# A hybrid decoder layer on one core: input loaded in four column pieces, unread products in the idle front, one Strassen block of the first FFN made plain

## The chip, the core and the metric

The kernel runs on one core of a Trainium2 chip. A core has a matrix engine (PE in the profile; its weight loads are PEld), a vector engine (DVE), a scalar engine (ACT), a general engine (POOL) and queues that start DMA transfers (SP's, and ACT's own). Each engine works through its own list of instructions in order and waits on semaphores. The metric is the device time of one execution in microseconds (us); lower is better.

## The reference, cut to what matters

One layer step for a prompt group (512 tokens) and a sample group (8 sequences of 4 tokens), 544 rows of width 1024 in all, in float32:

```python
def _layer(x, pos, p, attn_cache, ml_state):
    x = x + 0.5 * _swiglu(_rmsnorm(x, p['ffn1_norm']), p['ffn1_w_gate'], p['ffn1_w_up'], p['ffn1_w_down'])
    h = _rmsnorm(x, p['mix_norm'])
    # one projection, dilated attention (8 heads), mLSTM (4 heads), output projection
    ...
    x = x + mix @ p['w_out']
    x = x + 0.5 * _swiglu(_rmsnorm(x, p['ffn2_norm']), p['ffn2_w_gate'], p['ffn2_w_up'], p['ffn2_w_down'])
    return x, att_state, (C, n, m)
```

The hidden width of both FFNs is 2816, which is 22 column tiles of 128.

## The kernel before

The activations lie transposed: eight tiles `x` (128 of the 1024 columns by 544 rows). A float32 product is made of three products of rounded halves: the weight tile is split into `whi` (a cast on ACT) and `wlo` (a subtraction on DVE), the activation into `xh` and `xl`, and PE computes `xh*whi`, `xl*whi` and `xh*wlo`, each in two halves of 272 columns. One tile of 128 inputs (a `k`) of one column tile is therefore a group of six PE products, and a plain column tile (a `Job`) has eight groups, 48 products. Gate and up of one column tile are two jobs.

Two neighbouring column tiles can instead be one `Fast` job: gate and up of both by a Strassen scheme of seven products of 2x2 blocks, 7 x 24 = 168 PE products where four plain jobs take 192. It needs operands of its own (`oh`, `ol`, made from sums `xn`, `xd` on DVE and ACT) and sums of weights (`ws` on DVE). `PLAIN = 4` is the number of column tiles at the start of an FFN that are plain.

The FFN goes in parts of 8, 8 and 6 column tiles. The first part of FFN 1 is therefore 8 plain jobs, 2 `Fast` jobs and 8 down jobs.

The order of instructions on every engine is written by a planner when the program is built: class `Order` keeps a planned time `t` and clocks of the engines, pieces of work are generators that yield the time from which they may go on, and `Engine.cost` gives the planned cost of an instruction. These planned times fix only the order; on the chip, semaphores decide when an instruction starts.

The front works like this. SP's queue loads `ident`, the norm gain, the input as `xt` (per half of the 1024 columns four row blocks of 128x512, and `xst` for the samples), and between the halves the first two gate columns (`wraw`, 512 KB each). PE turns the input into `x` tiles by products with `ident` (four of `xt` and one of `xst` per tile). `FastNorm.from_rows` computes sums of squares from the rows (`sj`), `scales` makes the row scales and spreads them with a product of `dg` by `onesd` into `rb`; the gate's and up's results are multiplied by `rb` when they leave PSUM. PSUM has two accumulators for jobs (`mm`) and four small ones (`aux`). The first two jobs run interleaved:

```python
first = [(j, slot()) for j in jobs[:2]]
for ks in (range(0, 4), range(4, 8)):
    for i, (j, ps) in enumerate(first):
```

Of the kernel before, what the change touches and what calls it, by code (L numbers as in the profile page):

```python
# [51 lines left out]
class Order:  # L52
# [132 lines left out]
class Engine:  # L185
# [5 lines left out]
    def cost(self, op, out, ins, kw):  # L191
        n = max([size(out)] + [size(a) for a in ins])
        sbuf = all(a.space == bass.MemoryType.SB for a in [out] + ins)
        if self.name == "dma":
            b = 4 * size(out) * out.shape[0]
            return max(0.1, b / (3.6e5 if self.order.t > 15.0 else 2.7e5))
# [48 lines left out]
def hybrid_layer_kernel(ctx: ExitStack, tc: tile.TileContext, I: dict, C: dict, O: list):  # L245
# [49 lines left out]

    ident = small("ident", (P, P))
    dma.dma_start(ident, C["ident"])
    nc.scalar.preload_act_table_set("natural_log_exp_and_others")
    od.table = 1
    gcol = small("gcol", (P, 32))  # L300
    grow1 = small("grow1", (KD, P))
    dma.dma_start(grow1, I["ffn1_norm"].rearrange("(m p) -> m p", p=P))
# [63 lines left out]
    class FastNorm(Norm):  # L366
# [6 lines left out]
        def from_rows(self, blocks):  # L373
            self.rows = True
            ssa, ssd = small("ssa", (P, 2, 2)), small("ssd", (P, 3, 2))
            v, y, t = (small(n, (P, CH + 1)) for n in ("rsv", "rsy", "rst"))
            pool.memset(ssd, 1.0)
            for c in range(2):
                xb, xs_ = blocks[c]
                for b, x in enumerate(xb + [xs_]):  # L380
                    yield R(x) - 0.2
                    n = NS if b == CH else P
                    j = t2("sj", (P, 512))
                    if b < 2:
                        act.activation(j[0:n], x, AF.Square, accum_out=ssa[:, b, c:c + 1])
                    else:
                        dve.tensor_tensor_reduce(out=j[0:n], in0=x, in1=x, scale=1.0, scalar=0.0, op0=OP.mult,
                                                 op1=OP.add, accum_out=ssd[0:n, b - 2, c:c + 1])
            od.spawn(self.scales(ssa, ssd, v, y, t), 0, R(ssa, ssd) - 0.2)

        def scales(self, ssa, ssd, v, y, t):
            dve.tensor_tensor(v[:, 0:2], ssa[:, :, 0], ssa[:, :, 1], op=OP.add)
            dve.tensor_tensor(v[:, 2:5], ssd[:, :, 0], ssd[:, :, 1], op=OP.add)
# [99 lines left out]
    class Raw:  # L493


        def __init__(self, w, r0, nk, cols, *more):
            self.w, self.cols = w, cols
            self.parts = [(r0, nk)] + list(more)
            self.nk = sum(n for _, n in self.parts)
            self.left = len(cols)  # L500
            self.t = None

# [4 lines left out]
        def load_cols(self):  # L507
            c0, n = self.cols[0], len(self.cols)
            together = all(c == c0 + i * P for i, c in enumerate(self.cols))
            k0 = 0  # L510
            for r0, nk in self.parts:
                rows = self.w[r0:r0 + nk * P]
                if together:
                    dma.dma_start(self.t[:, k0:k0 + nk, :n * P], rows[:, c0:c0 + n * P].rearrange("(k p) c -> p k c", p=P))
                else:
                    for i, c in enumerate(self.cols):
                        dma.dma_start(self.t[:, k0:k0 + nk, i * P:(i + 1) * P],
                                      rows[:, c:c + P].rearrange("(k p) c -> p k c", p=P))
                k0 += nk

    class Job:
        def __init__(self, raw, c, xs, after, start=True, stop=True, split=None):
# [3 lines left out]
            self.w = None  # L526

        def split(self):
            hi = wp.tile([P, 8, P], F32R, name="whi", tag="wsp", bufs=8)
            lo = wp.tile([P, 8, P], F32R, name="wlo", tag="wsp", bufs=8)  # L530
            nk = self.nk
            if self.custom:
                self.custom(hi, lo)
            else:
                src = self.raw.t[:, :nk, self.c * P:(self.c + 1) * P]
                act.copy(hi[:, :nk], src)
                yield R(hi) - 0.3
                dve.tensor_tensor(lo[:, :nk], src, hi[:, :nk].bitcast(F32), op=OP.subtract)
                self.raw.left -= 1
            self.w = (hi, lo)  # L540
# [61 lines left out]
    def run(jobs):  # L602
# [19 lines left out]
        def splitter():  # L622
            for n, j in enumerate(jobs):
# [23 lines left out]
        def products(j, ps, ks, hs=(0, 1)):  # L647
            od.need(lambda: j.w is not None)
            hi, lo = j.w
            for k in ks:  # L650
                od.need(lambda: j.xs(k) is not None)
# [40 lines left out]
        for ks in (range(0, 4), range(4, 8)):  # L692
            for i, (j, ps) in enumerate(first):
                for k in ks:
                    products(j, ps, (k,))
                    used[0] = max(used[0], k + 1)
                    od.poll()
                if 7 in ks:
                    finish(j, ps)
                    at[0], unit[0] = i + 1, pos[i + 1]  # L700
# [16 lines left out]
    def ffn_jobs(pre, get_norm, after):  # L717
        wg, wu, wd = I[pre + "_w_gate"], I[pre + "_w_up"], I[pre + "_w_down"]
        jobs = []
        for f0, f1 in zip(PARTS, PARTS[1:]):  # L720
# [4 lines left out]
            def gate(f, zg=zg):  # L725
                def post(ps, full):
                    z = t2("zg")
                    yield 0, 0, lambda: get_norm().rb is not None
                    dve.tensor_tensor(halves(z), ps, halves(get_norm().rb), op=OP.mult)
                    done(full, kind="mm")  # L730
# [13 lines left out]
            def up(f, zg=zg, hidden=hidden):  # L744
                def post(ps, full):
# [5 lines left out]
                    dve.tensor_tensor(z, zg[f], z, op=OP.mult)  # L751
                    yield from hidden(f, z)
# [65 lines left out]
            for f in range(0, nf, 2):  # L818
                c0 = (f0 + f) * P
                if f0 + f >= PLAIN:  # L820
# [7 lines left out]
                else:  # L828
                    jobs += [Job(Raw(wg, 0, 8, [cols[i]]), 0, xs, gate(f + i)) for i in range(2)]
# [22 lines left out]

    xp4 = I["x_prompt"].rearrange("(b p) d -> p b d", p=P)
    xsm = I["x_sample"].flatten_outer_dims()
    xin = []
    for c in range(2):
        xs_ = t2("xst", (NS, 512))
        blocks = []
        for b in range(CH):
            xb = t2("xt", (P, 512))  # L860
            dma.dma_start(xb, xp4[:, b, c * 512:(c + 1) * 512])
            blocks.append(xb)
        dma.dma_start(xs_, xsm[:, c * 512:(c + 1) * 512])
        xin.append((blocks, xs_))
        if c == 0:
            jobs[0].raw.load()
            jobs[1].raw.load()
    jobs[2].raw.load()

    def start():  # L870
# [5 lines left out]
        for c in range(2):  # L876
            blocks, xs_ = xin[c]
            for m in range(4):
                x = t2("x")
                yield R(xs_, *blocks), 2, lambda: 4 * c + m < used[0] + 4  # L880
                pa, pb_ = aux(), aux()
                for b in range(CH):
                    tr(pa[:, b * P:(b + 1) * P], blocks[b][:, m * P:(m + 1) * P], ident)
                tr(pb_[:, 0:NS], xs_[:, m * P:(m + 1) * P], ident[0:NS, 0:NS])
                yield R(pb_) - 0.3
                copy(x[:, 0:S], pa)
                copy(x[:, S:N], pb_[:, 0:NS])
                xT[4 * c + m] = x
                done(pa, pb_)
                od.spawn(n1.add(4 * c + m), 0)  # L890
# [3 lines left out]
    od.spawn(n1.from_rows(xin), 2)  # L894
# [1001 lines left out]
```

## Time and profile before

| | |
|---|---|
| median of 3 runs | 1126.86 us (1126.65 to 1127.28) |
| profiled execution | 1127.17 us, of which the span from first to last instruction is 1125.4 us |
| PE | 1102.8 us busy, 98% of the span |
| DVE, ACT | 68% and 45% busy |

A row of the timeline is: start, duration, engine, line of the kernel, operation, `output<-inputs`, count of merged instructions, and in brackets the idle time before it with what ended it. The duration of a PE row reaches to the modelled end of the last product in it and overlaps the next row, so the pace of products is read from starts. A float32 product that is not of rounded halves (`ident`, `onesd`) shows as one or two records.

### The profile page before, as it was taken

The page shows a single profiled execution, that of the slowest core. Times are in us where ns is not written, and L with a number is a line of the kernel's source. Part 1 is how long each engine was busy: PE and PEld are TensorE (multiplying, and loading weights), DVE is VectorE, ACT ScalarE, POOL GpSimd, SP SyncE. Part 2 cuts the span into 40 slices and gives each one's busy share as a digit, 9 for nine tenths or more (in the row PEclk, how much of TensorE's full clock was granted, in tenths as well). Part 3 has the DMA queues.
Part 4 walks back from the last instruction along what each step waited for, and adds up shares of the span by engine and source line. Part 5 has one row for each costly group of instructions (what it writes and reads, how often), then busy time and mean ns, then how long its engine had stood idle before and what let it go on. Part 6 is the DMA issues. An engine that isn't in the chain of part 4 may idle for free. (4 is left out here: it accounts for less than half of the span.)

```text
span 1125.4 us, 21401 instructions
## 1 busy us (share of the span) xinstructions
PE 1102.8 (98%) x8819; PEld 1050.6 (93%) x8819; DVE 768.4 (68%) x1232; ACT 504.3 (45%) x900; POOL 95.6 (8%) x105
## 2 busy tenths in 40 slices
PE   7999999999999999999989999999999999999998
PEld 6999999999999999988876869999999999999997
DVE  6888337873487678689786537778962687537752
ACT  5555215451245446455653535454541355314541
POOL 0000000000000000165563010000000000000000
PEclk9999999999999999999999999999999999999999
DMA  7305312432143465675979563342242122422232
GB/s 231 102 15 159 105 38 76 149 114 78 36 140 99 124 215 134 189 227 161 316 227 331 189 215 113 97 148 76 76 134 92 61 91 75 150 76 76 66 105 60
DMA packets 143229, 145.34 MB, mean 129 GB/s; under 512 B 8868, under 2 KB 120772, under 8 KB 143132
## 3 DMA queue, kind: packets, MB, share of 16 engines
q1 hardware_dynamic: 143068, 143.98, 41.2%
q8 instruction: 69, 1.13, 0.4%
q14 instruction: 28, 0.23, 0.1%
q0 software_dynamic: 64, 0.00, 0.0%
HBM read 132.54 MB, written 9.18 MB: 126 GB/s over the span
## 5 line engine op out<-in xcount | busy, mean ns | idle before, releaser
L223 ACT CAST whi<-wraw 128x1024 fp32r<-128x1024 f32 (+3 forms) x180 | 174.1, 988 | 121.0 <-PE mm L282 93.5
L223 DVE TENSOR_TENSOR wlo<-wraw,whi 128x1024 fp32r<-128x1024 f32 (+3 forms) x180 | 210.2, 1176 | 20.4 <-ACT whi L223 20.2
L282 PE MATMUL mm<-oh,wlo 128*128 128x272 f32 x720 | 209.3, 291 | 2.2 <-DVE wlo L223 2.0
L282 PE MATMUL mm<-oh,whi 128*128 128x272 f32 x720 | 207.6, 288 | 0.1
L282 PE MATMUL mm<-ol,whi 128*128 128x272 f32 x720 | 207.2, 288 | 0.0
L282 PE MATMUL mm<-xh,whi 128*128 128x272 f32 x720 | 157.8, 301 | 0.0
L282 PE MATMUL mm<-xh,wlo 128*128 128x272 f32 x720 | 149.5, 289 | 0.2 <-DVE wlo L223 0.2
L282 PE MATMUL mm<-xl,whi 128*128 128x272 f32 x720 | 149.5, 289 | 0.0
L282 PE MATMUL mm<-hh,whi 128*128 128x272 f32 x704 | 147.3, 289 | 0.5 <-DVE x L223 0.5
L282 PE MATMUL mm<-hh,wlo 128*128 128x272 f32 x704 | 146.4, 288 | 0.0
L282 PE MATMUL mm<-hl,whi 128*128 128x272 f32 x704 | 146.3, 288 | 0.0
L223 DVE SCALAR_TENSOR_TENSOR x<-mm,x 128x544 f32<-128x544 f32 (+1 forms) x49 | 34.9, 713 | 158.1 <-PE mm L282 158.1
L282 PEld LDWEIGHTS mm<-oh,wlo 128*128 128x128 f32 x720 | 135.4, 188 | 5.5 <-DVE wlo L223 4.4
L282 PEld LDWEIGHTS mm<-oh,whi 128*128 128x128 f32 x720 | 135.5, 188 | 0.3 <-issue 0.3
L282 PEld LDWEIGHTS mm<-ol,whi 128*128 128x128 f32 x720 | 135.6, 188 | 0.0
L282 PEld LDWEIGHTS mm<-xh,whi 128*128 128x128 f32 x720 | 112.8, 190 | 12.4 <-issue 11.4
L282 PEld LDWEIGHTS mm<-xh,wlo 128*128 128x128 f32 x720 | 113.6, 189 | 0.5 <-DVE wlo L223 0.5
L282 PEld LDWEIGHTS mm<-xl,whi 128*128 128x128 f32 x720 | 113.6, 189 | 0.1
L282 PEld LDWEIGHTS mm<-hh,whi 128*128 128x128 f32 x704 | 110.6, 188 | 0.9 <-DVE x L223 0.8
L282 PEld LDWEIGHTS mm<-hh,wlo 128*128 128x128 f32 x704 | 110.9, 188 | 0.0
L282 PEld LDWEIGHTS mm<-hl,whi 128*128 128x128 f32 x704 | 110.7, 188 | 0.0
L223 ACT CAST whi<-ws 128x1024 fp32r<-128x1024 f32 x54 | 56.7, 1051 | 104.1 <-DVE ws L223 104.0
(324 smaller groups left out, 1772.2 us busy)
## 6 DMA issues: line engine op xcount, KB each, us to landing
wraw<-in_ffn_w_gate_dram SPq DMA_DIRECT2D x40, 512.0 KB
wraw<-in_ffn_w_up_dram SPq DMA_DIRECT2D x36, 512.0 KB
wraw<-in_ffn_w_down_dram SPq DMA_DIRECT2D x16, 1024.0 KB
kv<-in_cache_k_win_dram SPq DMA_DIRECT2D x56, 256.0 KB
kv<-in_cache_v_win_dram SPq DMA_DIRECT2D x56, 256.0 KB
wraw<-in_w_in_dram SPq DMA_DIRECT2D x16, 512.0 KB
wraw<-in_ffn_w_down_dram SPq DMA_DIRECT2D x8, 768.0 KB
wraw<-in_w_in_dram SPq DMA_DIRECT2D x6, 1024.0 KB
```

The lines of the kernel that those rows point to most:

```text
L223: r = fn(*args, **kw)
L282: nc.tensor.matmul(out, lhsT, rhs, start=start, stop=stop, **kw)
```

## The change

It does six things. (1) The input comes in four pieces of 256 columns (one DMA of 512 KB each, into buffers of the `wsp` pool that weight halves use later) instead of eight row blocks; between them stand the first gate column in two halves and the second one whole. `ident`, the gain and `xst` go through ACT's DMA queue ahead of ACT's table load. (2) Where the planner would let its time jump while it waits in the front, it now emits `filler()`: a product of `onesd` with 64 of its columns into a corner of an accumulator whose first real product overwrites it; nobody reads it. (3) The first two jobs are interleaved in finer steps. (4) The squares are taken per 256 columns, on whichever of ACT and DVE is free in the plan, and summed with a reduction. (5) Where `rb` is not yet there, a gate result is copied out of PSUM by ACT and multiplied later. (6) FFN 1 has six plain column tiles instead of four (`6 if pre == "ffn1" else PLAIN`), and the split of its hidden tiles waits until job 10. FFN 2's first gate column is also loaded and split in two halves. The planner's start values and its DMA rate for the first 15 us are set anew.

```diff
-        self.t = 0.0
-        self.clock = {"act": 0.0, "dve": 0.0, "pool": 0.0, "dma": 0.0, "hw": 0.0}
+        self.t = 0.8
+        self.clock = {"act": 3.1, "dve": 0.8, "pool": 0.8, "dma": 0.0, "hw": 0.0}
+        self.filler = None
...
-        self.t = min(later)
+        while self.filler and self.t < min(later) - 0.15:
+            self.filler()
+        self.t = max(self.t, min(later))
...
+    for n, (t, a) in enumerate([(ident, C["ident"]), (grow1, I["ffn1_norm"].rearrange("(m p) -> m p", p=P))]
+                               + [(xst[c], xsm[:, c * 512:(c + 1) * 512]) for c in range(2)]):
+        nc.scalar.dma_start(t, a)
+        od.ready[t.tensor.name] = (2.4 + 0.5 * n, "dma")
     nc.scalar.preload_act_table_set("natural_log_exp_and_others")
...
+            for t, (a, b) in zip(self.raw.at, self.raw.pieces):
+                src = self.raw.t[:, a:b, self.c * P:(self.c + 1) * P]
+                yield t - 0.1
+                act.copy(hi[:, a:b], src)
                 yield R(hi) - 0.3
+                dve.tensor_tensor(lo[:, a:b], src, hi[:, a:b].bitcast(F32), op=OP.subtract)
...
+                    if n in (2, 3):
+                        yield 0, 0, lambda: not any(reads[2 * n - 4:2 * n - 2])
...
+        def filler():
+            mm(first[1][1][:, 1, 3 * P:4 * P - 64], onesd, onesd[:, 0:64], skip_group_check=True)
+
+        od.filler = filler
+        for i, ks in ((0, (0, 1)), (0, (2, 3)), (1, (0, 1, 2, 3)), (0, (4, 5)), (1, (4, 5)), (0, (6, 7)), (1, (6, 7))):
...
+                    if get_norm().rb is None:
+                        src = halves(z)
+                        act.copy(src, ps)
+                        done(full, kind="mm")
+                        yield 0, 0, lambda: get_norm().rb is not None
+                    dve.tensor_tensor(halves(z), src, halves(get_norm().rb), op=OP.mult)
...
+                    if pre == "ffn1":
+                        yield 0, 0, lambda: at[0] >= 2 * PLAIN + 2 
                     yield from hidden(f, z)
...
-                if f0 + f >= PLAIN:
+                if f0 + f >= (6 if pre == "ffn1" else PLAIN):
                     jobs.append(Fast(Halves((wg, wu), 0, c0), Halves((wg, wu), 4 * P, c0), op, both(f)))
...
+    for c in range(4):
+        xb = wp.tile([P, CH, 256], F32, name="xt", tag="wsp", bufs=8)
+        dma.dma_start(xb, xp4[:, :, c * 256:(c + 1) * 256])
+        xin.append(xb)
+        if c < 2:
+            jobs[c].raw.load()
     jobs[2].raw.load()
```

PE's list from its first instruction, before: the gain's turn, then four input tiles (the first half of the columns) and the first group of products.

```order
L287 MATMUL aux<-ident,grow_75 128x8
L287 MATMUL aux<-ident,xt 128x128 x4
L287 MATMUL aux<-ident,xst 128x32
...
L282 MATMUL mm<-xh,whi 128x272 x2
L282 MATMUL mm<-xl,whi 128x272 x2
L282 MATMUL mm<-xh,wlo 128x272 x2
```

In the "..." the pair of `xt` and `xst` rows stands three times more. PE's list of the changed kernel at the same place (rows `mm<-onesd` are the unread products):

```order
L285 MATMUL mm<-onesd 128x64 x8
L290 MATMUL aux<-ident,grow_73 128x8
L285 MATMUL mm<-onesd 128x64 x5
L290 MATMUL aux<-ident,xt 128x128 x4
L290 MATMUL aux<-ident,xst 128x32
...
L285 MATMUL mm<-onesd 128x64 x12
...
L285 MATMUL mm<-xh,whi 128x272 x2
L285 MATMUL mm<-xl,whi 128x272 x2
L285 MATMUL mm<-xh,wlo 128x272 x2
```

Two input tiles stand ahead of the twelve unread products and two behind them; then come two groups of job 0, two tiles, two groups of job 0, two tiles, and the other twelve groups of jobs 0 and 1 without a break. 25 unread products are new; before, ten of the sixteen groups stood ahead of the products of `dg`, and now all sixteen and six more.

SP's DMA list, before and then changed, from its start:

```order
L223 DMA ident<-in_c_ident_dram 128x128
L223 DMA grow_75<-in_ffn_norm_dram 8x128
L223 DMA xt<-in_x_prompt_dram 128x512 x4
L223 DMA xst<-in_x_sample_dram 32x512
L223 DMA wraw<-in_ffn_w_gate_dram 128x8x128 x2
L223 DMA xt<-in_x_prompt_dram 128x512 x4
```

```order
L226 DMA xt<-in_x_prompt_dram 128x4x256
L226 DMA wraw<-in_ffn_w_gate_dram 128x4x128 x2
L226 DMA xt<-in_x_prompt_dram 128x4x256
L226 DMA wraw<-in_ffn_w_gate_dram 128x8x128
L226 DMA xt<-in_x_prompt_dram 128x4x256 x2
L226 DMA wraw<-in_ffn_w_up_dram 128x8x256
```

The input now opens the queue, and 768 KB (a piece and half a gate column) stand ahead of all that the first products need, where 2 MB of input and weights stood. Last, DVE's list where the first `Fast` job's weights are made, before and then changed (`hl` is the low half of a hidden tile, `zu` the up result):

```order
L223 TENSOR_TENSOR wlo<-wraw,whi 128x1024
L223 TENSOR_TENSOR ws<-wraw 128x1024
L223 TENSOR_TENSOR ol<-xn,oh 128x544
L223 TENSOR_TENSOR xd<-xn,xd 128x544
L223 TENSOR_TENSOR hl<-zu,hh 128x544
L223 TENSOR_TENSOR zu<-mm,rb 128x544
L223 TENSOR_TENSOR wlo<-ws,whi 128x1024
L223 TENSOR_TENSOR ws<-ws,wraw 128x1024
L223 TENSOR_TENSOR ol<-xd,oh 128x544
```

```order
L226 TENSOR_TENSOR wlo<-wraw,whi 128x1024
L226 TENSOR_TENSOR ws<-wraw 128x1024
L226 TENSOR_TENSOR hl<-zu,hh 128x544
L226 TENSOR_TENSOR zu<-mm,rb 128x544
L226 TENSOR_TENSOR wlo<-ws,whi 128x1024
L226 TENSOR_TENSOR ws<-ws,wraw 128x1024
L226 TENSOR_TENSOR zu<-zg,zu 128x544
L226 TENSOR_TENSOR wlo<-ws,whi 128x1024
```

The operand rows `ol` and `xd` no longer stand between the weight rows; they are made during the plain jobs ahead.

## Rows read from the trace of the kernel before

**Rows 1.** The page, part 1: busy time, share of the span and instructions of PE and DVE; part 2: PE's busy tenths and granted clock in 40 slices.

```profile
PE 1102.8 (98%) x8819; PEld 1050.6 (93%) x8819; DVE 768.4 (68%) x1232; ACT 504.3 (45%) x900; POOL 95.6 (8%) x105
PE   7999999999999999999989999999999999999998
PEclk9999999999999999999999999999999999999999
```

**Rows 2.** Busy time by stretch over the front: stretch, its length, busy us (and instructions) of each engine, granted clock, DMA share, GB/s.

```profile
0.00:5.00 5.00, 0.24 (x1) 0.18 (x1) 0.34 (x3) 1.30 (x2) 0.58 (x7) 1.00 0.43 136
5.00:10.00 5.00, 3.39 (x11) 1.83 (x11) 2.18 (x8) 2.39 (x6) 0.00 (x0) 1.00 0.90 270
10.00:15.00 5.00, 4.79 (x19) 3.68 (x19) 4.27 (x8) 4.58 (x8) 0.00 (x0) 1.00 1.08 331
15.00:20.00 5.00, 5.00 (x27) 4.04 (x25) 4.72 (x10) 4.32 (x11) 0.00 (x0) 1.00 1.10 347
20.00:25.00 5.00, 5.00 (x39) 4.75 (x39) 4.26 (x15) 2.79 (x8) 0.00 (x0) 1.00 0.69 217
```

**Rows 3.** The timeline of PE in the front.

```profile
8.04 0.48 PE L287 MATMUL aux<-ident,xt 128*128 128x128 f32 x1 [0.20 <-DMA xt<-in_x_prompt_dram]
8.68 1.11 PE L287 MATMUL aux<-ident,xt 128*128 128x128 f32 x4
9.97 1.11 PE L287 MATMUL aux<-ident,xt 128*128 128x128 f32 x4
...
14.65 0.66 PE L282 MATMUL mm<-xh,whi 128*128 128x272 f32 x2
15.10 0.65 PE L282 MATMUL mm<-xl,whi 128*128 128x272 f32 x2
...
16.01 1.06 PE L287 MATMUL aux<-ident,xt 128*128 128x128 f32 x4
...
19.45 0.60 PE L287 MATMUL aux<-ident,xt 128*128 128x128 f32 x4
20.16 0.52 PE L282 MATMUL mm<-xh,whi 128*128 128x272 f32 x2
...
23.07 0.41 PE L282 MATMUL mm<-xh,wlo 128*128 128x272 f32 x2
23.32 0.41 PE L282 MATMUL mm<-xh,whi 128*128 128x272 f32 x2
...
26.45 1.05 PE L282 MATMUL aux<-dg,onesd 128*128 128x128 f32 x8
27.77 0.52 PE L282 MATMUL mm<-xh,whi 128*128 128x272 f32 x2
```

**Rows 4.** The timeline in the first `Fast` job: its first product, and the three places at which PE's starts lie further apart, with DVE's weight halves.

```profile
68.44 0.29 PE L282 MATMUL mm<-oh,whi 128*128 128x272 f32 x1
...
71.41 1.23 DVE L223 TENSOR_TENSOR ws<-ws,wraw 128x1024 f32<-128x1024 f32 x1
72.55 0.72 DVE L223 TENSOR_TENSOR ol<-xd,oh 128x544 fp32r<-128x544 f32 x1
72.67 1.05 ACT L223 CAST whi<-ws 128x1024 fp32r<-128x1024 f32 x1 [0.40 <-DVE ws L223]
74.46 1.22 DVE L223 TENSOR_TENSOR wlo<-ws,whi 128x1024 fp32r<-128x1024 f32 x1
74.58 0.29 PE L282 MATMUL mm<-ol,whi 128*128 128x272 f32 x1
75.73 0.39 PE L282 MATMUL mm<-oh,wlo 128*128 128x272 f32 x1 [0.86 <-DVE wlo L223]
75.96 0.29 PE L282 MATMUL mm<-oh,whi 128*128 128x272 f32 x1
78.72 0.29 PE L282 MATMUL aux<-ol,whi 128*128 128x272 f32 x1
79.40 0.39 PE L282 MATMUL aux<-oh,wlo 128*128 128x272 f32 x1 [0.39 <-DVE wlo L223]
82.38 0.28 PE L282 MATMUL mm<-ol,whi 128*128 128x272 f32 x1
82.88 0.39 PE L282 MATMUL mm<-oh,wlo 128*128 128x272 f32 x1 [0.21 <-DVE wlo L223]
```

**Rows 5.** The timeline of PE at a small float32 product with a full weight tile (four products of 16 columns, eight records) and the row behind it.

```profile
623.84 0.96 PE L282 MATMUL aux<-c_sel,pmk 128*128 128x16 f32 x8
624.65 0.50 PE L282 MATMUL mm<-xh,whi 128*128 128x272 f32 x2
```

**Rows 6.** Busy time by stretch around PE's one long wait later in the kernel (columns as in rows 2).

```profile
588.00:592.00 4.00, 1.25 (x24) 0.34 (x13) 4.00 (x6) 1.57 (x5) 2.35 (x2) 1.00 0.30 94
592.00:596.00 4.00, 3.85 (x23) 3.16 (x24) 3.48 (x10) 0.00 (x0) 1.27 (x1) 0.57 0.92 306
```

**Rows 7.** The timeline: ACT's table load and SP's first DMA issues.

```profile
0.74 1.28 ACT L298 ACT_TABLE_LOAD   x1 [0.74 <-PEq L1880]
0.74 0.40 SPq L223 DMA_DIRECT2D ident<-in_c_ident_dram  x1
1.61 1.78 SPq L223 DMA_DIRECT2D xt<-in_x_prompt_dram  x4
```

**Rows 8.** The chain that ended last, at the change from the output projection to FFN 2: start, length, what, count.

```profile
712.42 31.55 PE mm L282 x252
```

More of the change, by code (lines that the diff above doesn't have):

```diff
@@ L371, in __init__, with from_rows @@
             self.ops = {}
-        def from_rows(self, blocks):
+        def from_rows(self, blocks, last):
             self.rows = True
-            ssa, ssd = small("ssa", (P, 2, 2)), small("ssd", (P, 3, 2))
-            v, y, t = (small(n, (P, CH + 1)) for n in ("rsv", "rsy", "rst"))
[L377 to L389, printed above, removed]
@@ L391, in scales @@
-        def scales(self, ssa, ssd, v, y, t):
-            dve.tensor_tensor(v[:, 0:2], ssa[:, :, 0], ssa[:, :, 1], op=OP.add)
-            dve.tensor_tensor(v[:, 2:5], ssd[:, :, 0], ssd[:, :, 1], op=OP.add)
+            sums = {e: small("ss" + e, (P, CH + 1, 4)) for e in ("act", "dve")}
+            for t in sums.values():
+                pool.memset(t, 0.0)
+            work = [(R(x) - 0.2, x[:, b], P, b, c) for c, x in enumerate(blocks) for b in range(CH)]
+            work += [(R(x) - 0.2, x, NS, CH, c) for c, x in enumerate(last)]
@@ L501, in __init__ @@
             self.t = None
+            self.pieces = [(0, self.nk)]
         def load(self):
@@ L727, in post @@
                     z = t2("zg")
[L728 to L730 removed]
+                    src = ps
+                    if get_norm().rb is None:
[4 more added lines that the diff above has]
+                    dve.tensor_tensor(halves(z), src, halves(get_norm().rb), op=OP.mult)
+                    if src is ps:
+                        done(full, kind="mm")
                     yield R(z) - 0.5
@@ L828, in ffn_jobs @@
                 else:
-                    jobs += [Job(Raw(wg, 0, 8, [cols[i]]), 0, xs, gate(f + i)) for i in range(2)]
+                    rg = Raw(wg, 0, 4, cols[:1], (4 * P, 4)), Raw(wg, 0, 8, cols[1:])
+                    rg[0].pieces = [(0, 4), (4, 8)]
+                    jobs += [Job(rg[i], 0, xs, gate(f + i)) for i in range(2)]
                 jobs += [Job(ru, i, xs, up(f + i)) for i in range(2)]
@@ L851, in hybrid_layer_kernel @@
     last_fast = max(n for n, j in enumerate(jobs) if isinstance(j, Fast))
+    reads = [2 + CH] * 4
     xp4 = I["x_prompt"].rearrange("(b p) d -> p b d", p=P)
-    xsm = I["x_sample"].flatten_outer_dims()
     xin = []
[L856 to L867, printed above, removed]
+    for c in range(4):
[4 more added lines that the diff above has]
+            jobs[c].raw.load()
     jobs[2].raw.load()
@@ L875, in start @@
         done(pg_)
[L876 to L890, printed above, removed]
+        for m in range(KD):
+            blocks, xs_ = xin[m // 2], xst[m // 4]
+            x = t2("x")
+            yield R(xs_, blocks), 2, lambda: m < used[0] + 4
+            pa, pb_ = aux(), aux()
+            for b in range(CH):
+                tr(pa[:, b * P:(b + 1) * P], blocks[:, b, m % 2 * P:(m % 2 + 1) * P], ident)
+            reads[m // 2] -= 1
+            tr(pb_[:, 0:NS], xs_[:, m % 4 * P:(m % 4 + 1) * P], ident[0:NS, 0:NS])
+            yield R(pb_) - 0.3
+            copy(x[:, 0:S], pa)
+            copy(x[:, S:N], pb_[:, 0:NS])
+            xT[m] = x
+            done(pa, pb_)
+            od.spawn(n1.add(m), 0)
         yield 0
     od.spawn(start(), 1)
-    od.spawn(n1.from_rows(xin), 2)
+    od.spawn(n1.from_rows(xin, xst), 2)
     rb = lambda: n2.rb
```

66 lines of the change are left out of this document (41 added, 25 removed).

## The prediction

> **What bounds the kernel now.** I read the page first: PE is busy 98% of the span and falls short in the first slice, a little in the middle and in the last [rows 1]. So time is PE's work plus the stretches in which PE waits or runs slowly, and the change must be priced there. The table by stretches shows how little PE gets done early: 11, 19 and 27 records per 5 us, then 39 [rows 2]. The timeline gives the reason [rows 3]. Until 8.04 us PE waits for input rows. From there it is nearly always occupied, but slow: pairs of 272-column products start 0.45 us apart at 14.65 and 15.10 and 0.25 us apart at 23.07 and 23.32. [...] The granted-clock column says 1.00 for the front [rows 2], so it has no record of this and the starts must be read. Four turns of input take 1.06 us at 16.01 and 0.60 at 19.45: the level rose between the two, after PE had run from 14 us on with hardly a gap. That it falls after idleness is seen once: PE was busy 1.25 of 4 us, and the next stretch shows 0.57 [rows 6].
>
> **Where the front ends now.** Jobs 0 and 1 are 96 products. That of 27.77 us is the 61st (ten groups stand ahead of it), and the first `Fast` product starts at 68.44 [rows 3, 4]: 8 x 48 - 60 = 324 products in 40.67 us, 0.1255 each, so nothing stalls between. Job 1 therefore ends at 27.77 + 36 x 0.1255 = 32.29; without the `dg` products (26.45 to 27.77, needed in both kernels) at **30.97 us**. That is the number to beat.
>
> **The front after.** The first tiles need the first piece and the small inputs, 0.72 MB. When does it land? In the rows 0.68 MB have moved by 5 us and 270 GB/s follow [rows 2], so the 1.12 MB up to the fourth row block had moved by 6.6, and PE had that block at 8.04 [rows 3]: 1.4 behind. The input now opens SP's queue, 0.87 us earlier than its 1.61 [rows 7]. 0.72 MB moved by 5.2, plus 1.4, less 0.87: at most 5.7; I take 5.4. ACT's four DMA issues at about 0.4 each and its table load of 1.28 [rows 7] end near 3.7 and are hidden under this wait; held up by 2 us they would delay ACT's first copy.
>
> Two tiles at half clock cost 1.29 each (8.68 to 9.97): 8.0 us. Then twelve unread products. The nearest row is four float32 products of 16 columns: eight records in 0.81 us, 0.20 per product at the full level [rows 5], far more than 16 columns need, so it looks like a cost per instruction. At half clock the lower bound is 0.21 (a turn of 128 columns takes (1.11 - 0.48) / 3 = 0.21 per record [rows 3]; half the columns, two records); the upper bound is twice the row, 0.40. I take 0.21, nearest the row: 2.5 us, to 10.5. The 13 unread products ahead of the input cost 2.7 from about 1 us on and lie under the wait for it; at 0.40 they would end at 6.5 and delay it by 1.
>
> From there I take the full level, since PE has then run from 5.4 on with no gap but those between tiles. A tile costs 0.71 (19.45 to 20.16) to 0.8, a group six times 0.125, 0.75. Six tiles 4.8 and sixteen groups 12.0: **27.3 us**, if the operands are there. The third and fourth pieces are wanted at 13.6 and 16.7; their 2.82 and 3.35 MB had moved by 12.4 and 14.0 at the rates of the rows [rows 2], plus 1.4 less 0.87, so 12.9 and 14.5. A split on DVE behind a full `wlo` (1.22 [rows 4]) may cost up to 0.9 once. Gain of the front: 30.97 - 27.3 = **3.7**, between 5.4 and -1.9 (both under the rivals).
>
> The rows show that turns by `ident` filled most of the time from 16.0 to 19.4 in which the level rose [rows 3], so turns did not hinder it, and the sum above ends at 1124.4. [...]
>
> **The plain block.** Two column tiles as four plain jobs are 192 products instead of 168: 24 x 0.1255 = **+3.0**, all on PE's path. Against it, the replaced block waited for `wlo`: starts lie 1.15, 0.68 and 0.50 us apart instead of 0.125, and each resumption costs 0.1 more (75.73 to 75.96): 1.13 + 0.66 + 0.48 = **-2.3** [rows 4]. On DVE `ol` and `xd`, 0.72 each, stood between the weight halves, and the chain of `ws` (1.23), cast (1.05) and `wlo` (1.22) is 3.5 us long [rows 4] where a Strassen step is 24 x 0.125 = 3.0. The remaining block has the chain without the operand rows. Its second step's weights start about 1 us ahead; three more steps lose 0.5 each, and two rows of about 0.7 still stand between: I give it **+0.5**, bounds 0 and 2.3.
>
> **Edits at nothing.** ACT's copy of a gate result frees job 0's accumulator while job 1's last two groups (1.5 us) run; without that cover job 2 starts late by the copy. The squares in 18 pieces lengthen ACT's and DVE's lists ahead of `rb`, which is wanted only when job 2's result leaves, 6 us after job 1. FFN 2's first column in halves lies under PE's 252 products in 31.55 us, 0.1252 each, without a wait [rows 8].
>
> **The sum.** -3.7 + 3.0 - 2.3 + 0.5 = -2.5. The profiled execution took 1127.17 us (span 1125.4 and 1.8 around it) and would take 1124.7; it is 0.3 above the median, so the forecast for a median is **1124.4**. About 0.2%, 2.25 us, is what a measurement of this kernel can tell from no change; the forecast lies just past it.
>
> **Rivals.**
> *The clock stays down (slower).* With unread products at 0.40 and half clock until two groups have passed: the input waits until 6.5, two tiles to 9.1, twelve products to 13.9, two tiles to 16.5, two groups at 1.36 to 19.2; then at the full level four tiles 3.2 and fourteen groups 10.5, 32.9. The front loses 1.9 and the sum is +3.1: 1130.0. With products at 0.21 it ends at 29.5, 1126.6. What decides is where the level rises: each tile and group at half clock costs about 0.5, and from about 17 us on the change is slower. For it: PE turned input from 8.04 to 12 in the rows without reaching the full level. Against it: those turns had gaps, and the level did rise in a stretch that was mostly turns.
> *Nothing gained (same).* The pieces land no earlier than the row blocks do, the fourth at 16 to 18, or the remaining `Fast` block keeps its 2.3: each costs 1 to 2, 1125.5 to 1127. For it: only 270 GB/s moved from 5 to 10 us; against it: 331 and 347 in the next stretches [rows 2].
> *More gained.* The 13 early products raise the level before the first tile: two tiles 1.6 instead of 2.6, the first piece at 4.7, so the front ends at 25.6, and the block loses nothing: 1122.2.
>
> **Numbers.** Likeliest 0.47 (1123.0 to 1125.6, two thirds of it past the bound), more gained 0.20, nothing gained 0.20, clock down 0.13 (nearly all past the bound). Faster by over 0.2%: 0.31 + 0.20 = 0.51; slower by over 0.2%: 0.12; same 0.37. The range leaves out about a tenth at either end: 1121.4 to 1128.0.
>
> **What would show it.** Right: a pace of 0.25 us from the first groups on, job 0's first product near 12, jobs 0 and 1 done near 27, `dg` some 4.5 us later, the single `Fast` block with at most one start gap over 0.3 us, and waits as now behind 120 us. Wrong: `mm<-onesd` records 0.2 us apart, a pace of 0.45 beyond 15 us, PE waiting for `xt` behind the twelve, or waits for `wlo` in the plain jobs, which the sum holds at nothing.

## The result, and the profile after

The changed kernel is slower: a median of 1132.96 us (1130.02 to 1134.14, six runs) against 1126.81 us (1125.11 to 1127.39, six runs), a ratio of 1.0050 (95% interval 1.0034 to 1.0066), some 6 us. The forecast was 1124.4, with 1128.0 as its upper end. The profiled execution took 1133.3 us, its span 1131.5.

The page after, part 1 and PE's row of part 2, to be laid beside [rows 1]:

```profile
PE 1114.4 (98%) x8893; PEld 1064.3 (94%) x8893; DVE 759.5 (67%) x1231; ACT 501.8 (44%) x905; POOL 95.6 (8%) x106
PE   9999999999999999999998999999999999999998
```

PE is 11.6 us busier in a span that is 6.1 longer: idle time in front is filled, and work, or slow work, was added beyond it. Two rows say where. They are the products of FFN 1's hidden tiles and FFN 2's, in the list of what touches `hh`; the two numbers behind the durations are the starts of the first and of the last one. The kernel before:

```profile
L282 PE MATMUL mm<-hh,whi x704: 282/288/394, 113.0 to 1119.6; 128*128 128x272 f32 x176
```

The kernel after:

```profile
L285 PE MATMUL mm<-hh,whi x704: 282/287/393, 121.3 to 1126.0; 128*128 128x272 f32 x176
```

The first of these products, where the down jobs of FFN 1's first part begin, starts 8.3 us later, and the last one, at the kernel's end, 6.4 later. So the whole loss, and 2 us more, lies ahead of 121 us.

**The front.** The table by stretches, as [rows 2]:

```profile
15.00:20.00 5.00, 5.00 (x22) 4.21 (x22) 2.96 (x5) 2.51 (x5) 0.00 (x0) 1.00 0.25 69
20.00:25.00 5.00, 4.85 (x29) 4.03 (x29) 2.73 (x4) 3.04 (x6) 0.00 (x0) 1.00 0.72 214
```

From 5.2 us on PE is occupied almost throughout and gets less done than before: 22 records between 15 and 20 us where there were 27, 29 in the next 5 us where there were 39. DMA moves only 69 GB/s between 15 and 20 us, and no row of PE below waits for a piece of the input, so the input isn't what PE lacks. The timeline of PE, as [rows 3]:

```profile
1.06 3.68 PE L285 MATMUL mm<-onesd 128*128 128x64 f32 x16 [1.06 <-DVE epsc L226]
5.24 0.24 PE L290 MATMUL aux<-ident,grow 8*128 8x8 f32 x1 [0.51 <-DMA grow<-in_ffn_norm_dram]
5.41 2.40 PE L285 MATMUL mm<-onesd 128*128 128x64 f32 x10
7.60 1.06 PE L290 MATMUL aux<-ident,xt 128*128 128x128 f32 x4
...
10.12 5.38 PE L285 MATMUL mm<-onesd 128*128 128x64 f32 x24
15.29 1.06 PE L290 MATMUL aux<-ident,xt 128*128 128x128 f32 x4
...
17.81 0.82 PE L285 MATMUL mm<-xh,whi 128*128 128x272 f32 x2
18.43 0.65 PE L285 MATMUL mm<-xl,whi 128*128 128x272 f32 x2
18.89 0.66 PE L285 MATMUL mm<-xh,wlo 128*128 128x272 f32 x2
...
20.70 1.06 PE L290 MATMUL aux<-ident,xt 128*128 128x128 f32 x4
...
21.93 0.66 PE L290 MATMUL aux<-ident,xt 128*128 128x128 f32 x4
...
26.18 0.52 PE L285 MATMUL mm<-xh,whi 128*128 128x272 f32 x2
```

The same first group in the kernel before:

```profile
12.54 0.82 PE L282 MATMUL mm<-xh,whi 128*128 128x272 f32 x2
```

The twelve unread products, two records each, run from 10.12 to 15.29: 0.43 us each. The first group stands at 17.81, where it stood at 12.54. Its pairs are 0.45 us apart (18.43 to 18.89); four turns still take 1.06 at 20.70 and 0.66 at 21.93. So the level rises near 22 us, where in the kernel before it rose between 16.0 and 19.4 [rows 3]. By the level I mean the pace of the starts: pairs of 272-column products 0.45 us apart at the lower one, which the prediction calls half clock, and 0.25 at the upper. In the front the granted-clock column reads 1.00 at both [rows 2], so that the clock sets the pace there is my reading; later in the kernel before, the column shows 0.50 between 594 and 595 us, and the pairs stand 0.46 apart (594.37 and 594.83). From 26.18 on 72 products remain, at 0.1255: jobs 0 and 1 end at **35.2**, 4.2 later than the 30.97 before.

**The plain block.** PE and DVE around the one `Fast` block that is left, as [rows 4]:

```profile
92.42 0.73 DVE L226 TENSOR_TENSOR ol<-xd,oh 128x544 fp32r<-128x544 f32 x1 [6.63 <-PE mm L285]
93.06 2.63 DVE L226 TENSOR_TENSOR hl<-zu,hh 128x544 fp32r<-128x544 f32 x4
...
97.00 1.22 DVE L226 TENSOR_TENSOR wlo<-wraw,whi 128x1024 fp32r<-128x1024 f32 x1
97.02 0.29 PE L285 MATMUL mm<-ol,whi 128*128 128x272 f32 x1
98.27 0.40 PE L285 MATMUL mm<-oh,wlo 128*128 128x272 f32 x1 [0.96 <-DVE wlo L226]
98.50 0.29 PE L285 MATMUL mm<-oh,whi 128*128 128x272 f32 x1
...
101.81 0.39 PE L285 MATMUL aux<-oh,wlo 128*128 128x272 f32 x1 [0.26 <-DVE wlo L226]
...
105.41 0.39 PE L285 MATMUL mm<-oh,wlo 128*128 128x272 f32 x1 [0.32 <-DVE wlo L226]
...
109.01 0.39 PE L285 MATMUL aux<-oh,wlo 128*128 128x272 f32 x1 [0.32 <-DVE wlo L226]
...
112.48 0.40 PE L285 MATMUL mm<-oh,wlo 128*128 128x272 f32 x1 [0.21 <-DVE wlo L226]
```

The first `wlo` begins at 97.00, when PE already has the block's first product behind it (96.90): behind four rows of `hl`, 2.63 us, that stand together in DVE's list, and a row of `ol` ahead of them (0.64 by starts), at which DVE had waited 6.63 us for PE. From 97.02 to 98.27 PE waits. Each later wait is longer than its bracket says, since the starts before and behind it lie further apart too. By starts, the way the 2.3 of the replaced block was counted, it is 1.22 for the first and 0.53, 0.58, 0.58 and 0.46 for the others: **3.4** in all. The second block of the kernel before shows no wait. So the block costs 24 x 0.1255 = 3.0, less 2.3, plus 3.4: 4.1. With 4.2 of the front that is the 8.3 by which FFN 1's first part is late.

**What comes back.** The same instructions of DVE and ACT start 8.0 us later than before from 360 to 480 us and 6.2 later from 530 us on. Between the two the kernel before has waits at 503.55 (`Cst`, 0.39) and 526.03 (`smax`, 0.29) that the kernel after has not. The order of instructions there is the same in both; experiments below with the changed order have one or both of these waits again (that with turns both). At each of the two the distance shrinks, by 0.8 and by 1.1. They come and go from trace to trace, so I don't count this as a gain of the change; no run tested it.

### The profile page after: what moved, and what is told of

Read it like the earlier page. It is cut to its first block, busy times and chain, and to the rows that moved or that the text cites. A ratio compares the mean times of both kernels' runs of the same rounds, so it can differ in the third digit from the quotient of the medians.

```text
span 1131.5 us, 21560 instructions
## 1 busy us (share of the span) xinstructions
PE 1114.4 (98%) x8893; PEld 1064.3 (94%) x8893; DVE 759.5 (67%) x1231; ACT 501.8 (44%) x905; POOL 95.6 (8%) x106
## 5 line engine op out<-in xcount | busy, mean ns | idle before, releaser
L226 ACT CAST whi<-wraw 128x1024 fp32r<-128x1024 f32 (+4 forms) x182 | 174.6, 978 | 119.6 <-PE mm L285 92.4
L226 DVE TENSOR_TENSOR wlo<-wraw,whi 128x1024 fp32r<-128x1024 f32 (+4 forms) x182 | 210.7, 1165 | 21.7 <-ACT whi L226 21.4
L285 PE MATMUL mm<-oh,wlo 128*128 128x272 f32 x680 | 197.8, 291 | 2.5 <-DVE wlo L226 2.5
L285 PE MATMUL mm<-oh,whi 128*128 128x272 f32 x680 | 195.9, 288 | 0.0
L285 PE MATMUL mm<-ol,whi 128*128 128x272 f32 x680 | 195.6, 288 | 0.0
L285 PE MATMUL mm<-xh,whi 128*128 128x272 f32 x784 | 171.3, 300 | 0.0
L285 PE MATMUL mm<-xl,whi 128*128 128x272 f32 x784 | 163.0, 289 | 0.2 <-DVE xl L226 0.2
L285 PE MATMUL mm<-xh,wlo 128*128 128x272 f32 x784 | 162.7, 289 | 0.0
L285 PEld LDWEIGHTS mm<-xh,whi 128*128 128x128 f32 x784 | 122.9, 190 | 12.3 <-issue 11.4
L285 PEld LDWEIGHTS mm<-xl,whi 128*128 128x128 f32 x784 | 123.8, 190 | 0.4 <-DVE xl L226 0.4
```

The costliest lines, as they stand in the source:

```text
L226: r = fn(*args, **kw)
L285: nc.tensor.matmul(out, lhsT, rhs, start=start, stop=stop, **kw)
```

## The experiments

The theory behind the first four runs: the unread products are dead time of 0.43 us each that adds nothing towards the level, and the plain block costs 4.1. All kernels below compute the layer in full. Each ratio is against the kernel before in the same round of runs, where its median was 1126.8, 1127.2, 1126.7 or 1126.4, so the ratios compare better than the medians. The diffs leave out the lines that keep the planner's count and those that set up `onesr`, `turn` and `dense`.

| run | median us (runs) | ratio to before (95%) | jobs 0 and 1 end |
|---|---|---|---|
| after | 1132.96 (6) | 1.0050 (1.0034 to 1.0066) | 35.2 |
| no unread products | 1129.33 (11) | 1.0016 (1.0006 to 1.0025) | 29.2 |
| dense unread products | 1124.37 (12) | 0.9978 (0.9966 to 0.9990) | 28.5 |
| after, four plain tiles | 1137.29 (4) | 1.0084 (1.0068 to 1.0100) | 34.9 |
| none, four plain tiles | 1131.85 (9) | 1.0041 (1.0025 to 1.0056) | 29.1 |
| dense, early ones alone | 1127.08 (12) | 0.9999 (0.9985 to 1.0012) | 27.1 |
| the same, hidden tiles earlier | 1125.17 (12) | 0.9985 (0.9972 to 0.9998) | 27.4 |
| turns instead | 1131.62 (1) | single run | 29.6 |
| narrow products of rounded halves | 1130.83 (1) | single run | 35.3 |
| before, six plain tiles | 1131.35 (6) | 1.0044 (1.0031 to 1.0057) | 30.7 |
| dense, hidden tiles earlier | 1125.01 (12) | 0.9980 (0.9968 to 0.9993) | 28.4 |
| dense, eight in the middle, hidden tiles earlier | 1124.40 (10) | 0.9977 (0.9968 to 0.9987) | 27.0 |
| before, dense unread products ahead | 1125.99 (11) | 0.9996 (0.9986 to 1.0005) | 29.5 |

### No unread products

```diff
-            mm(first[1][1][:, 1, 3 * P:4 * P - 64], onesd, onesd[:, 0:64], skip_group_check=True)
+            od.issue("pe", 64 / 595.0, [first[1][1][:, 1, 3 * P:4 * P - 64]], [onesd, onesd])
```

The planner still counts them, so all else keeps its place.

> The changed kernel with its 25 unread products left out; every other instruction stands in the same order. Theory (they are dead time): x2's turns start when the second piece lands, near 9.1 us instead of 15.29; four input tiles end near 11.7 instead of 17.81, the first group starts there, the level rises 4 to 6 us later (15.8 to 17.8), jobs 0 and 1 end near 29.0 instead of 35.2, and the time falls by about 6.2 to 1126.8 (1126 to 1128). Rival (the unread products bring the level forward, and without them it stays down): pairs still 0.45 us apart beyond 20 us, the front's end 31 or later, 1129 or more. Rival (the input is late): PE waits for the input until 15, 1132 or more.

```profile
9.23 1.09 PE L290 MATMUL aux<-ident,xt 128*128 128x128 f32 x4 [0.95 <-DMA xt<-in_x_prompt_dram]
...
11.78 0.82 PE L285 MATMUL mm<-xh,whi 128*128 128x272 f32 x2
...
15.89 0.66 PE L290 MATMUL aux<-ident,xt 128*128 128x128 f32 x4
...
20.14 0.52 PE L285 MATMUL mm<-xh,whi 128*128 128x272 f32 x2
```

In this timeline of PE the second piece releases x2 at 9.23, the first group starts at 11.78, the four turns at 15.89 already run at the upper level (0.66 us, against 1.05 at 14.66), and 20.14 + 9.04 = 29.2. The front is as expected: 6.0 us come back, and the level rises sooner without the unread products, not later. That rules out the late input and the rival by which they help. The time is 1129.3, though, not 1126.8. In the traces 2 us of the 6 are gone by 610 us: 0.7 between 515 and 580, and 1.3 behind a wait of 2.9 us for `mk` that both kernels have (it ends at 598.59 in the kernel after and at 593.20 here). Behind it the granted clock falls. The stretch in the kernel after, and in this one (the column behind POOL's is the granted clock):

```profile
588.00:606.00 18.00, 15.10 (x144) 12.05 (x138) 15.16 (x34) 7.41 (x26) 9.66 (x8) 0.91 0.63 204
```

```profile
588.00:606.00 18.00, 15.11 (x124) 10.55 (x123) 11.91 (x25) 4.64 (x15) 7.98 (x10) 0.81 0.85 293
```

0.91 against 0.81: its mean over the stretch is lower in this execution. In three other profiled executions (none with four plain tiles, early dense products alone, narrow products of rounded halves) the stretch shows 1.00. From the end of the wait to the first product of `c_sel`, 244 records on, it is 31.7 us in the kernels before and after, 33.0 here, and 30.3 to 33.1 over all traces. So these executions differ by over 2 us there; that the runs of one kernel lie apart for this reason is likely, but only one execution of each was profiled.

### Dense unread products

```diff
-            mm(first[1][1][:, 1, 3 * P:4 * P - 64], onesd, onesd[:, 0:64], skip_group_check=True)
+            for h in range(2):
+                nc.tensor.matmul(first[1][1][:, 1, :HN], onesr[:, :P], onesr, start=True, stop=True, skip_group_check=True)
```

`onesr` holds the constant of `onesd` as rounded halves, 272 columns of it.

> The changed kernel in which each unread product of 64 float32 columns is replaced by two unread products of rounded halves of 272 columns each, the shape of a group's products; order of all else the same. At half clock two of them take 2 x 0.227 = 0.45, the same as the 0.43 of what they replace. Theory (small products keep PE occupied but empty, dense ones raise the level): the level rises before 9 us, the middle twelve then cost 3.0 instead of 5.2, input tiles 0.75, and jobs 0 and 1 end near 28.5 instead of 35.2: 1126.3. Rival (unread work of any kind doesn't bring the level, only what follows the first group does): pairs 0.45 apart to the end of the unread products, the level near 22, front end 35.5, 1133.

```profile
1.54 3.84 PE L720 MATMUL mm<-onesr 128*128 128x272 f32 x16 [1.54 <-DVE epsc L226]
...
5.56 1.52 PE L720 MATMUL mm<-onesr 128*128 128x272 f32 x10
6.91 0.60 PE L290 MATMUL aux<-ident,xt 128*128 128x128 f32 x4
...
8.38 3.27 PE L720 MATMUL mm<-onesr 128*128 128x272 f32 x24
11.49 0.60 PE L290 MATMUL aux<-ident,xt 128*128 128x128 f32 x4
...
19.51 0.52 PE L285 MATMUL mm<-xh,whi 128*128 128x272 f32 x2
```

Sixteen products ahead of the gain's turn take 0.23 us each, ten behind it 0.135, and the first input tile is turned in 0.60. The level rose between 5 and 6 us and held through eight tiles of turns (four turns take 0.60 or 0.66 in each); the middle 24 cost 3.1 instead of 5.2. The front ends at 19.51 + 9.04 = 28.5, as expected, and the kernel is faster than before by 0.1 to 0.34%. An unread product can do what the prediction wanted of it; the one in the change can't.

### Turns, and narrow products

What is it in the 64-column product that fails: its type, its width, or that it isn't followed by real work? The dense run answers the last: no more real work follows its products than follows these. Two single runs are for the others. In the first the middle twelve are 24 unread turns and the early thirteen are left out; in the second all are rounded halves with 64 columns.

```diff
-            mm(first[1][1][:, 1, 3 * P:4 * P - 64], onesd, onesd[:, 0:64], skip_group_check=True)
+            for h in range(2 if turn[0] > 13 else 0):
+                nc.tensor.transpose(first[1][1][:, 1, HN:HN + P], onesd, ident)
```

`turn[0]` counts the places of unread products.

> The changed kernel without the 13 early unread products, and with 24 unread turns of 128 columns by ident in place of the middle 12: between 5.6 and some 16.8 us PE does nothing but turns, back to back. Theory (turns do not bring the level, dense products do): turns at 0.25 us each to the end, the level 4 to 5 us behind the first group at 16.8, so at 20.8 to 21.8, front end 34 or later. Rival (occupied is enough, as the prediction had it): turns fall from 0.25 to 0.15 us apart before 14, front end near 30.

```profile
8.02 4.71 PE L718 MATMUL mm<-ident,onesd 128*128 128x128 f32 x24
12.57 0.60 PE L290 MATMUL aux<-ident,xt 128*128 128x128 f32 x4
...
14.03 0.52 PE L285 MATMUL mm<-xh,whi 128*128 128x272 f32 x2
```

My theory fell here: PE had done nothing but turns from 5.45 us on, and at 12.57 four of them take 0.60. Single starts of the 24 lie 0.213 us apart up to 11.91 and 0.11 from 11.91 on. The first group, at 14.03, meets the upper level: its next pairs are 0.25 apart (14.39 and 14.64). In this trace turns by `nc.tensor.transpose` brought it; the prediction had read from [rows 3] that they don't hinder it.

```diff
+                nc.tensor.matmul(first[1][1][:, 1, HN:HN + 64], onesr[:, :P], onesr[:, :64], start=True, stop=True, skip_group_check=True)
```

> The changed kernel with each unread float32 product replaced by two unread products of rounded halves of 64 columns: the type of the dense ones, the width of the original. Theory (it is the columns streamed that count): a product costs some 0.1 to 0.2, set by its weight load, and the level still rises only 4 to 5 us behind the first group. Rival (it is the type): the level rises before 9 us as with 272 columns.

```profile
10.16 5.19 PEld L720 LDWEIGHTS mm<-onesr 128*128 128x128 f32 x24
10.16 5.33 PE L720 MATMUL mm<-onesr 128*128 128x64 f32 x24
...
18.94 0.66 PE L285 MATMUL mm<-xh,wlo 128*128 128x272 f32 x2
...
21.98 1.11 PE L290 MATMUL aux<-ident,xt 128*128 128x128 f32 x4
...
23.57 0.41 PE L285 MATMUL mm<-xl,whi 128*128 128x272 f32 x2
```

Twenty-four narrow products of rounded halves take 5.1 us (10.16 to 15.30), 0.214 each, as much as the records of the float32 ones, and the level rises near 23 us. The type made no difference, then; the shape did: this run and the dense one differ in width alone, 64 columns against 272. The price isn't set by the columns multiplied, since turns of 128 columns lie 0.213 apart too. The weight loads, of 128 columns in both, fill the stretch (5.19 us in the row of PEld), so my estimate is that the price is theirs. No run changes the loads alone. At the upper level a record with a full weight tile takes 0.10 [rows 5]; the 0.214 here is twice that.

### The plain block, taken apart

Four plain tiles in the changed kernel (the hold on hidden tiles goes with the six), and the same without unread products.

```diff
-                if f0 + f >= (6 if pre == "ffn1" else PLAIN):
+                if f0 + f >= PLAIN:
-                    if pre == "ffn1":
-                        yield 0, 0, lambda: at[0] >= 2 * PLAIN + 2 
```

> The changed kernel with four plain column tiles in FFN 1 as before, so two Strassen blocks; the front as changed. Theory (FFN 1's offset of 8.4 us splits into 4.25 of the front and 4.15 of the plain block, being 24 more products, 3.0, and stalls of 3.4 in the block that is left against 2.3 in the one replaced): front end at 35.2, waits for wlo in the first of two blocks alone, 1133.0 - 4.15 = 1128.9 (1128 to 1130). Rival (the plain block costs 1.2 as forecast, and the front has done the rest): 1131.8.

> Both: no unread products and four plain column tiles, that is the new loading and interleaving alone. Theory (the two costs add): 1133.0 - 6.2 - 4.15 = 1122.7 (1121.5 to 1124), faster than before by 0.3 to 0.4%, front end near 29 against 30.97. Rival (some of the loss was absorbed by the wait near 500 us, where the offset of the changed kernel to before fell from 8.0 to 6.2, so a gain ahead of it is worth less): 1124.5 to 1126.

Both came out the other way: 1137.3 and 1131.9, slower than with six. PE's waits between 30 and 130 us with four plain tiles, and two stretches of 4 us:

```profile
PE mm L285 <- DVE ol L226: 2.5, 2, 1.7
PE aux L285 <- DVE wlo L226: 1.2, 1, 1.2
```

```profile
92.00:96.00 4.00, 2.72 (x18) 2.08 (x16) 4.00 (x6) 1.08 (x2) 0.00 (x0) 1.00 0.84 266
96.00:100.00 4.00, 2.35 (x10) 2.35 (x11) 3.90 (x7) 1.98 (x3) 0.00 (x0) 0.52 0.05 11
```

PE waits for operands, not only for weights: with `wlo` of the `mm` products (0.5) and `oh` (0.4) 4.6 us in all, DVE is full, and behind the stretch in which PE was busy 2.72 of 4 us the granted clock is 0.52. The `dg` products start at 39.6 here and at 39.85 in the kernel after, against 26.45 before [rows 3]:

```profile
L285 PE MATMUL aux<-dg,onesd x8: 272/275/275, 39.6 to 40.3; 128*128 128x128 f32 x8
```

`rb`, and with it the operands `xn`, comes 13 us later. Without unread products and with four tiles `dg` starts at 33.8, and PE's waits are the same four rows: there too `dg` stands 4.6 us behind the end of jobs 0 and 1, where before it stood 4.5 ahead of it. With six plain tiles PE waits for `wlo` alone (2.1 us, bracketed, in the kernel after): they give that chain its time. So in this front they pay, though they cost PE what was said. In the old front they don't:

```diff
-                if f0 + f >= PLAIN:
+                if f0 + f >= (6 if pre == "ffn1" else PLAIN):
+                    if pre == "ffn1":
+                        yield 0, 0, lambda: at[0] >= 2 * PLAIN + 2
```

> The kernel before with six plain column tiles in FFN 1 and the hold on hidden tiles that goes with them, nothing else of the change. Theory (the plain block costs the same in either front: 3.0 for 24 more products, and 1.1 because the block that is left loses more than the one replaced): front end 30.97 as before, FFN 1 longer by 4.1, 1126.8 + 4.1 = 1130.9 (1130 to 1132). Rival (as forecast, +1.2): 1128.0. Rival (it pays in this front too, as it did against two blocks in the changed one): under 1126.8.

It took 1131.35, near the expected 1130.9. In the trace the block costs 3.4, not 4.1: the first `wlo` starts at 91.64, 0.57 us ahead of the block's first product, where in the kernel after it starts 0.1 behind, so that the first of the five waits is short (0.56 by starts instead of 1.22). DVE's list is the same in front of it but for the row of `ol`, which isn't there:

```profile
87.70 2.63 DVE L223 TENSOR_TENSOR hl<-zu,hh 128x544 fp32r<-128x544 f32 x4 [6.58 <-PE mm L282]
...
91.64 1.22 DVE L223 TENSOR_TENSOR wlo<-wraw,whi 128x1024 fp32r<-128x1024 f32 x1
```

The median lies 4.5 to 4.9 above the kernel before; what makes up more than the 3.4 isn't shown.

### Towards a faster version

Four kernels: dense products only ahead of the input (`if turn[0] <= 13`); the same with the split of two hidden tiles one job earlier; that with all dense products; and that with eight in the middle (`turn[0] <= 17`).

```diff
-                        yield 0, 0, lambda: at[0] >= 2 * PLAIN + 2 
+                        yield 0, 0, lambda: at[0] >= 2 * PLAIN + 2 - (f < 2)
```

> As the kernel with dense unread products, but only those ahead of the input (26 of 272 columns); the middle 24 are left out. Theory (the level, once raised by dense work ahead of the input, holds through the input's turns, and the middle ones are dead time there too): x2's turns start at the landing of the second piece, 9.2, instead of 11.49; a tile costs 0.75; the first groups run 11 to 13, jobs 0 and 1 end near 26.6 (26 to 27.5) instead of 28.55, and the time falls by about 2 from 1124.4 to 1122.4. Rival (without the middle ones the level falls again in the gap before the second piece or during the turns): groups 0.45 apart, the front's end 28.5 or later, 1124.5 or more.

> The one before, and the split of the first two hidden tiles may begin one job earlier, so that only two rows of hl, not four, stand together ahead of the Strassen block's weight halves on DVE. Theory (the block that is left loses 3.4, of which 1.2 because 2.63 us of hl delay its first wlo): the start gap of 1.25 at the second product's successor closes, the others (0.5 to 0.6 each) stay, 1.2 less than the kernel before: 1121.2. Rival (the rows of hl wait for buffers in any order, or the chain of weight halves sets all gaps): no change against it.

> Dense unread products at all 25 places (1124.4 in an earlier run) and the split of the first two hidden tiles one job earlier. Theory (the two gains add; the earlier hidden tiles closed the first start gap of the block, worth 1.6 in the trace): 1122.8 (1121.8 to 1124). Rival (with the middle products kept the hidden tiles gain nothing): 1124.4.

> As the one before, but of the middle dense products only eight are kept, which reach to the landing of the second piece near 9.2. Theory (eight are enough to keep the level in every execution, and the other sixteen are dead time, 1.5 in the trace): front end near 27.1, 1121.3, and a spread no wider than that with all of them. Rival (in some executions the level is not held with few of them, as the spread of 1123.6 to 1130.1 without any suggests): as slow as with all or slower, 1123 to 1125.

The block did as expected: with two rows of `hl` in front instead of four, PE's first long wait and one of the short ones are gone, and three are left, shown here from the run with the early products alone:

```profile
95.96 0.39 PE L285 MATMUL mm<-oh,wlo 128*128 128x272 f32 x1 [0.33 <-DVE wlo L226]
99.56 0.39 PE L285 MATMUL aux<-oh,wlo 128*128 128x272 f32 x1 [0.32 <-DVE wlo L226]
103.03 0.40 PE L285 MATMUL mm<-oh,wlo 128*128 128x272 f32 x1 [0.19 <-DVE wlo L226]
```

In the traces that is worth 1.6 us, and the shorter middle another 1.5 in the front. Little of it reached the end. With early products alone the fronts end near where they should (27.1 and 27.4), but the times are 1127.1 and 1125.2 where 1122.4 and 1121.2 were expected. The other two took 1125.0 and 1124.4 where 1122.8 and 1121.3 were expected; their ratios, 0.9980 and 0.9977, can't be told from the 0.9978 of dense products alone. In the traces the lead of 1.75 us that earlier hidden tiles have over dense products alone is 0.8 from 600 us on, and the 1.5 of the shorter middle is 0.4: it goes between 500 and 570 us, where DVE is busy 19.8 of 20 us (520 to 540) and PE waits for it now here, now there. That a sooner start meets a full DVE there fits, but was not tested by itself. Nor was the spread without middle products (1123.6 to 1130.1, against 1122.0 to 1125.4 with eight): its profiled execution held the level (pairs 0.25 apart at 11.51 and 11.76), and whether others lost it stays open. The slowest of the twelve has a mean granted clock of 0.946 on record and the others 0.996 to 0.999, but not where in the run. The fastest versions, dense products at all places, and eight in the middle with hidden tiles earlier, are 0.22 and 0.23% faster than before.

Last, dense products alone, 34 of them at the head of PE's list in the kernel before:

```diff
+    for _ in range(34):
+        nc.tensor.matmul(dense[:, 1, :HN], onesr[:, :P], onesr, start=True, stop=True, skip_group_check=True)
```

> The kernel before with 34 dense unread products of 272 columns ahead of everything on the matrix engine, nothing else. Theory (dense work raises the level some 4 us after its start, and turns with short waits hold it): the level near 6 instead of 18.7, input tiles at 0.75; the first groups still wait for weight halves to 13.5 and the second half of the input lands at 15.3, so jobs 0 and 1 end near 29.2 instead of 30.97: 1125.1. Rival (PE's waits between the landings let the level fall): groups 0.45 apart, no gain, 1126.8 or more.

The front gains 1.5 in the trace, near the 1.8 expected; PE waits for weight halves in its place (0.43 for `whi`, 0.96 for `wlo` in the first group). The time, 1125.99 with an interval that reaches to 1.0005, can't be told from no change.

## Why the prediction was wrong

**The unread products** are where it failed. I took 0.21 each, as the nearest row gave 0.20 at the full level, and halved for the width. The row was the right one and had been read: a cost per instruction. It has two records of 0.10 each, and at the lower level each takes 0.213, so 0.43 per product, past even the upper bound of 0.40. The twelve cost 5.2 instead of 2.5. The thirteen in front ended at 7.60 instead of lying under the wait for input, forecast to end at 5.4. So the third tile begins at 15.29 instead of 10.5: 4.8 of the 7.9 us by which the front missed.

**"From there I take the full level"** is the step that failed outright, and it cost the other 3.1: from 15.29 the rest takes 19.9 instead of 16.8. It rested on PE having run from 5.4 us on with no gap but those between tiles. PE did so, and had run from 1.06 on but for 0.51 us, and the level still rose only near 22 us, behind the first two groups. That PE is shown as occupied said nothing of the level here. No run shows that the lower level of the front is half the clock; what the runs show is pairs 0.45 and 0.25 us apart, a ratio of 1.8, and turns 0.213 and 0.11 apart, a ratio of 1.9. The argument about turns was right and didn't help, since it was carried over to products of another shape, of which no row showed anything about the level. With dense products the front comes out at 28.5, near the 27.3 forecast. Most of the sum's front was thus right for a change that wasn't made.

**The rival "the clock stays down"** named what happened, a lower pace for longer, and the price of 0.40, and gave 32.9 and 1130.0. It was given 0.13. It still let the level rise after two groups from 16.5 on; they stood at 17.81, one more tile ran slowly, and the front ended at 35.2. Two of the prediction's own signs of being wrong came true: records 0.2 us apart, and a pace of 0.45 beyond 15 us.

**The plain block.** +3.0 and -2.3 stand. The remaining block's own stalls were +0.5, with 2.3 as the bound; they are 3.4. "About 1 us ahead" was said of the second step's weights, and it was the first step's that were late: the hold on the hidden tiles, which the change list names, lines up four rows of `hl` in front of them, and one row of `ol` stands with them. I had priced the two rows between later steps and not what the hold gathers ahead of the first. Front and block together missed by 10.8 us; 1.8 of it came back between 480 and 530 us.

**Edits at nothing.** No wait for the gate results or `xt` showed up. But "`rb` is wanted only when job 2's result leaves" looked at the wrong user. `dg` came 13.4 us later, not 4.5, and the operands of the `Fast` blocks hang on it. With six plain tiles that is covered but for the row of `ol`; with four it costs 4.6 us of waits, and behind them the granted clock shows 0.52. The squares in pieces, the copied gate results and FFN 2's halves weren't run by themselves, so what each adds to the late `dg` stays open.

**The landings** held: the first piece is there at 4.96, and without unread products the first tile starts at 5.64, where 5.4 was taken, and the second piece is there by 9.23. No input tile of the changed kernel waits for its piece.

## What to carry to other kernels

Fill an idle matrix engine only with the shape of product that you know to move the level, and look at its price at the lower level, which is the one that it ran at here; two unread products of the groups' own shape cost about what one narrow float32 product does (0.45 and 0.43 us) and do the work. Where a change puts off a chain of small steps (here the row scales), follow it to every reader and not only to the next. A wait in the planner that holds work back to one point lines it up in front of whatever comes at that point.

## What was not expected of the hardware

A record of 64 columns takes 0.213 us at the lower level, float32 or rounded halves alike, as long as one of 128, and 17 us of little else than such products and turns (1.06 to 17.81, with 0.5 us of waiting) did not raise the level, while 26 products of 272 columns, from 1.54 us on, had raised it before 7. Turns alone, back to back from 8.02 to 12.57 behind two turned tiles, raised it too. From 588 to 606 us, where the wait of 2.9 us for `mk` stands, the granted clock was 0.81, 0.91 or 1.00 in different profiled executions.
